# Decoder trunk on one core: gate, q and k turned and stored one token tile at a time, their splits and the scores in later slots, three more warming matmuls

## The chip, the core and the metric

The kernel runs on one core of a Trainium2 chip. The metric is the device time of one execution in microseconds; lower is better. The engines are named as in the profile: PE is TensorE (PEld its weight loads), DVE is VectorE, ACT is ScalarE, POOL is GpSimd and SP is SyncE. Each engine works through its own instructions in a fixed order and waits where an input is not there; POOL and SP also issue DMAs, in that order.

## What is computed

A trunk of two layers over 256 tokens of width 2048, in float32. In each layer:

```
h = rmsnorm(x, g) @ w_in            # columns: q, k, v and a gate z
q, k = rope(q), rope(k)
o = attention(q, k, v)              # per head, causal
x = x + (o * silu(z)) @ w_out
```

Layer 0 has two kinds of heads: 8 dilated heads (a mixture of three windows, which the kernel computes as one masked softmax), and 4 differential heads `(softmax(q1 k1) - lam * softmax(q2 k2)) @ v` with a norm behind them. Layer 1 has 16 causal heads. A last rmsnorm gives the output.

## The kernel before

**Slots and chunks.** The two layers are cut into 40 chunks of 512 output columns, in the order of `layer_chunks` (line 33): v, q, k, z for group 0, then q, k, z, v for groups 1 to 3, then four chunks of the output projection. A group is four heads (or two differential pairs). A chunk is 16 slots, one for each block of 128 of the 2048 inputs. Float32 products are made from three matmuls on parts rounded to a shorter format (high times high, high times low, low times high), and there are two token tiles of 128, so a slot is 6 matmuls of 128x512.

**Weights.** SP loads 1 MB pieces (`raw`, 3 buffers). `split(m)` (line 101) makes the parts of one 1024-column piece, enough for two slots: ACT writes `wh` (line 122), DVE writes `wl` (line 123). There are four buffers of each, so that the split for a slot pair 2m, 2m+1 can run only when the pair four earlier has been used; it is ahead of its use by six slots at most. In what follows a split "for slot s" is the one with 2m = s.

**Work in the slots.** Everything else is put into slots by `at(slot, f)` and runs after that slot's matmuls. What a chunk leaves is scheduled from `nxt`, the slot behind its end (lines 531 to 569). The Tile framework then orders the instructions of each engine by its own estimate of when inputs are ready, so an instruction can stand earlier or later than its slot; that order is fixed when the program is built.

**The path of q, k and z to the scores.** `evac_rope` (line 262) applies the rotation on DVE, four instructions for a token tile (lines 270 to 273), and `turn` (line 233) transposes 32x32 blocks (line 235). Both token tiles go into one tile `bz`; behind the second, `place` (line 238) stores it to DRAM by one DMA of 512 KB (`dt`, line 243) and reads it back transposed by eight DMAs of 64 KB (line 247), all on POOL, the loads waiting for the store to land. `split_rope` (line 278) splits q and k: ACT writes `qh`, `kh` (line 285), DVE `ql`, `kl` (line 286), one token tile after the other for k. `evac_z` (line 250) sends the gate along the same path to the tile `u`.

**Scores and products.** `softmax` (line 314) starts with a matmul on unsplit k and q of the first token tile (line 317) and goes on with three on the split parts. `attn_t` (line 349) transposes the probabilities through DRAM, a store `d` (line 356) and four loads `p` (line 360) for a head; `attn_h` splits them (`th`, `tl`, lines 369 and 370); `attn_o` and `diff_o` multiply by v; `finish_y` (line 384) multiplies by the gate and writes `yh`, `yl`, which the output projection reads. Evacuations are put at nxt and nxt + 2, the split of q and k at nxt + 13, the scores of a head at nxt + 14 and on.

**The start.** `WARM` (line 26) matmuls of 128x128 on ones (line 137) run on PE while the first loads are under way. Each is two passes, so the profile counts 20.

Of the kernel before, what the change touches and what calls it, by code (L numbers as in the profile page):

```python
# [8 lines left out]
F32 = mybir.dt.float32  # L9
# [6 lines left out]
P = 128  # L16
S = 256
# [5 lines left out]
SCALE = HD ** -0.5  # L23
LAM_INIT = 0.8 - 0.6 * math.exp(-0.3 * 0)
AHEAD = 3
WARM = 10
RAW_BUFS = 3
SPLIT_BUFS = 4
ALIGN = 512
# [23 lines left out]
def trunk(ctx, tc, x_nat, x_t, w0, o0, w1, o1, g0, g1, gfin, lam, subln, cos_t, sin_t,  # L53
          mask_d, mask_c, ident_in, out):
    nc = tc.nc
# [6 lines left out]
    work = ctx.enter_context(tc.tile_pool(name="work", bufs=1))  # L62
# [3 lines left out]
    dram = ctx.enter_context(tc.tile_pool(name="dram", bufs=2, space=bass.MemoryType.DRAM))  # L66
# [68 lines left out]
    pw = patt.tile([P, P], F32, tag="O", name="pw")  # L135
    for i in range(WARM):
        nc.tensor.matmul(pw, ones, ones, start=True, stop=True)
# [5 lines left out]
    def xr(kt):  # L143
        return xraw[kt // 4][:, kt % 4]
# [13 lines left out]
    md = const.tile([P, 3 * P], F32, name="md")  # L158
    mc = const.tile([P, 3 * P], F32, name="mc")
# [67 lines left out]
    def at(slot, f, *a):  # L227
        fill.setdefault(slot, []).append((f, a))

    yh, yl = [], []  # L230
    U, Q, K, V = {}, {}, {}, {}

    def turn(src, bt, tt):

        nc.vector.transpose(bt[:, :, tt].rearrange("p c h j -> p h c j"),  # L235
                            src.rearrange("p (h c j) -> p h c j", h=4, c=4))

    def place(bt, name):


        t = work.tile([P, 2, 4, 4, 32], F32, tag=name, name=name)
        d = dram.tile([P, 4, S], F32, tag="dt", name="dt")
        nc.gpsimd.dma_start(d, bt.rearrange("p c t h j -> p c (t h j)"))  # L243
        dv = d.rearrange("(a i) c (t x) -> c t i a x", a=4, t=2)
        for tt in range(2):
            for c in range(4):
                nc.gpsimd.dma_start(t[32 * c:32 * c + 32, tt].rearrange("p a h j -> p a (h j)"), dv[c, tt])  # L247
        return t

    def evac_z(ps, layer, g, tt, box):  # L250
        if tt == 0:
            box["bt"] = work.tile([P, 4, 2, 4, 32], F32, tag="bz", name="bz")
        z = work.tile([P, CW], F32, tag="t1", name="zt")
        th = work.tile([P, CW], F32, tag="t2", name="zth")
        nc.scalar.activation(z, ps[:, tt], AF.Copy, scale=rn[:, tt:tt + 1])
        nc.scalar.activation(th, z, AF.Tanh, scale=0.5)
        nc.vector.scalar_tensor_tensor(z, th, 1.0, z, op0=ALU.add, op1=ALU.mult)
        turn(z, box["bt"], tt)
        if tt == 1:
            U[layer, g] = place(box["bt"], "u")  # L260

    def evac_rope(ps, name, store, layer, g, tt, box):
        if tt == 0:
            box["bt"] = work.tile([P, 4, 2, 4, 32], F32, tag="bz", name="bz")
        t1 = work.tile([P, CW], F32, tag="t1", name="rt1")
        t2 = work.tile([P, CW], F32, tag="t2", name="rt2")
        r, n = rn[:, tt:tt + 1], HD // 2
        p4, a4, b4 = (x.rearrange("p (h d) -> p h d", h=4) for x in (ps[:, tt], t1, t2))
        co, si = (x[:, tt, None, :].to_broadcast([P, 4, HD]) for x in (cosN, sinN))
        nc.vector.scalar_tensor_tensor(a4, p4, r, co, op0=ALU.mult, op1=ALU.mult)  # L270
        nc.vector.scalar_tensor_tensor(b4[:, :, 0:n], p4[:, :, n:HD], r, si[:, :, 0:n], op0=ALU.mult, op1=ALU.mult)
        nc.vector.scalar_tensor_tensor(b4[:, :, n:HD], p4[:, :, 0:n], r, si[:, :, n:HD], op0=ALU.mult, op1=ALU.mult)
        nc.vector.tensor_add(t1, t1, t2)
        turn(t1, box["bt"], tt)
        if tt == 1:
            box["t"] = place(box["bt"], name)

    def split_rope(name, store, layer, g, box):

# [233 lines left out]
    for (kind, layer, g), slot0 in list(zip(chunks, starts))[:-1]:  # L513
        ps = pacc.tile([P, 2, CW], F32, tag="acc", name=f"acc{slot0}")
        nxt = slot0 + KT
        for slot in range(slot0, nxt):
            if slot % 2 == 0:
                split(slot // 2 + AHEAD)
                load((slot // 2 + AHEAD) // 2 + 1)
            if layer == 0 and slot < KT and 2 * AHEAD <= slot + 4 < KT:  # L520
                split_x(0, slot + 4, xr(slot + 4))
            wh, wl = (x[slot % 2] for x in splits[slot // 2])
            kt = slot - slot0
            for b in range(2):
                bs = slice(b * P, (b + 1) * P)
                a_h, a_l = (yh[kt][:, bs], yl[kt][:, bs]) if kind == "o" else \
                    (xhl[kt][:, 0, bs], xhl[kt][:, 1, bs])
                mm3(ps[:, b], a_h, a_l, wh, wl, start=kt == 0, stop=kt == KT - 1)
            for f, a in fill.pop(slot, []):
                f(*a)  # L530
        if kind in "zqk":
            box = {}
            for tt in range(2):
                if kind == "z":
                    at(nxt + 2 * tt, evac_z, ps, layer, g, tt, box)
                else:
                    at(nxt + 2 * tt, evac_rope, ps, kind, (Q, K)[kind == "k"], layer, g, tt, box)
            if kind != "z":
                at(nxt + 13, split_rope, kind, (Q, K)[kind == "k"], layer, g, box)
            if kind != "k":  # L540
                continue
            if layer == 0 and g >= 2:
                for h in range(2):
                    box = {}
                    at(nxt + 14 + 6 * h, diff_s, layer, g, h, box, 0)
                    at(nxt + 16 + 6 * h, diff_s, layer, g, h, box, 1)
                    at(nxt + 18 + 6 * h, attn_t, box)
                    at(nxt + 32 + 5 * h, attn_h, box, True)
                    at(nxt + 34 + 5 * h, diff_o, layer, g, h, box)
                    at(nxt + 38 + 5 * h, diff_y, layer, g, h, box)  # L550
            else:
                for h in range(4):
                    box = {}
                    at(nxt + 14 + 3 * h, attn_s, layer, g, h, md if layer == 0 else mc, box)
                    at(nxt + 17 + 3 * h, attn_t, box)
                    at(nxt + 32 + 2 * h, attn_h, box)
                    at(nxt + 34 + 2 * h, attn_o, layer, g, h, box)
        elif kind == "v":
            if slot0 == 0:
                at(nxt + 5, evac_v, ps, layer, g)  # L560
            else:
                evac_v(ps, layer, g)
        else:
            evac_o(ps, layer, g)
            if layer == 0:
                at(nxt + 3, next_x, g, 0)
                at(nxt + 6, next_x, g, 1)
            else:
                at(nxt + 4, times_g, g)
# [64 lines left out]
```

## Time and profile before

| | us |
|---|---|
| median of 3 runs (lowest, highest) | 1003.44 (997.42, 1008.15) |
| the profiled execution's own time | 999.49 |
| its span, first to last instruction | 997.7 |
| PE busy | 942.4 |
| DVE busy | 643.0 |
| ACT busy | 474.5 |
| POOL busy | 200.5 |
| mean granted TensorE clock | 0.971 of full speed |

The profile is of one execution. Its span leaves out 1.8 us of its time. A group in the list of costliest groups gives the line, the engine, output and inputs, shape and count, then the busy time in us, the mean duration in ns, and the idle time just before these instructions with what ended it. Matmuls overlap, so the interval from one to the next, not their duration, is what they cost. In the timeline each row has the start, the duration, the engine and the instruction, with idle time before it in brackets. The rows on which the prediction rests stand in it.

### The profile page before, as it was taken

To read this page: it belongs to the slowest core of one execution; us is meant where nothing else is said; L and a number is where in the kernel's file an instruction comes from. 1 tells how busy PE (TensorE), PEld (TensorE's weight loads), DVE (VectorE), ACT (ScalarE), POOL (GpSimd) and SP (SyncE) were. 2 spreads that over 40 slices of the span, in tenths; PEclk is the share of its full clock that TensorE was granted. 3 is DMA by queue.
4 is the path that set the end of the run, shared out by engine and by line. 5 is a ranking of instruction groups with operands and counts; after the bars stand their busy time and mean duration, and the time that the engine had idled before them with its cause. 6 is when DMAs were issued, how large, how long until landed. Compare 5 with 4: busy or idle time off the path is not lost. (4 is left out here: it accounts for less than half of the span.)

```text
span 997.7 us, 11928 instructions
## 1 busy us (share of the span) xinstructions
PE 942.4 (94%) x4276; PEld 778.8 (78%) x4276; DVE 643.0 (64%) x999; ACT 474.5 (48%) x711; POOL 200.5 (20%) x368
## 2 busy tenths in 40 slices
PE   8999997999799988999999999979996999799996
PEld 7887886888688867888888878868885888587886
DVE  6666875756566666665555768747664766575572
ACT  7534643553355335554554454535442644264451
POOL 0021441321113110300000125215011421132000
PEclk9999999999989998999999999989997999899999
DMA  9786776566645664655555668667665756676542
GB/s 329 259 320 232 242 241 212 198 210 244 214 161 210 213 232 137 220 196 174 187 193 185 237 212 266 219 199 234 212 209 180 245 198 211 211 241 227 187 169 84
DMA packets 42827, 213.21 MB, mean 214 GB/s; under 512 B 9040, under 2 KB 9808, under 8 KB 22672
## 3 DMA queue, kind: packets, MB, share of 16 engines
q1 hardware_dynamic: 27504, 175.21, 50.1%
q0 software_dynamic: 14976, 36.20, 11.4%
q10 hardware_dynamic: 288, 1.05, 0.3%
q8 instruction: 33, 0.54, 0.2%
q14 instruction: 26, 0.21, 0.1%
HBM read 192.23 MB, written 20.19 MB: 213 GB/s over the span
## 5 line engine op out<-in xcount | busy, mean ns | idle before, releaser
L312 PE MATMUL acc<-wh,x 128*128 128x512 f32 x2048 | 655.1, 397 | 1.6 <-ACT wh L119 1.6
L123 DVE TENSOR_TENSOR wl<-raw,wh 128x1024 fp32r<-128x1024 f32 x314 | 382.7, 1220 | 206.1 <-ACT wh L122 205.3
L122 ACT ACTIVATE wh<-raw 128x1024 fp32r<-128x1024 f32 x314 | 332.0, 1059 | 359.8 <-PE acc L312 322.2
L312 PEld LDWEIGHTS acc<-wh,x 128*128 128x128 f32 x2048 | 390.7, 191 | 81.9 <-ACT wh L119 1.8
L312 PE MATMUL acc<-wl,x 128*128 128x512 f32 x1024 | 405.1, 396 | 0.2 <-DVE wl L120 0.2
L312 PEld LDWEIGHTS acc<-wl,x 128*128 128x128 f32 x1024 | 196.0, 191 | 39.8 <-DVE wl L120 0.5
L312 PE MATMUL acc<-wh,yh 128*128 128x512 f32 x224 | 88.3, 394 | 0.0
L312 PE MATMUL acc<-wl,yh 128*128 128x512 f32 x224 | 87.4, 390 | 0.0
L312 PE MATMUL acc<-wh,yl 128*128 128x512 f32 x224 | 87.3, 390 | 0.0
L243 POOL DMA_DIRECT2D dt<-bz x24 | 13.6, 568 | 305.6 <-DVE bz L235 302.1
L360 POOL DMA_DIRECT2D p<-d x112 | 61.2, 554 | 56.8 <-DMA d<-bt 29.5
L317 PE MATMUL ps_s<-k,q 128*128 128x128 f32 x64 | 14.7, 315 | 41.8 <-DMA k<-dt 41.6
L317 PEld LDWEIGHTS ps_s<-k,q 128*128 128x128 f32 x64 | 12.8, 214 | 47.0 <-issue 29.8
L312 PEld LDWEIGHTS acc<-wh,yl 128*128 128x128 f32 x224 | 42.0, 188 | 9.1 <-DVE yl L389 0.3
L312 PEld LDWEIGHTS acc<-wl,yh 128*128 128x128 f32 x224 | 42.1, 188 | 8.4
L312 PEld LDWEIGHTS acc<-wh,yh 128*128 128x128 f32 x224 | 42.1, 188 | 8.2
L247 POOL DMA_DIRECT2D q<-dt x64 | 34.7, 550 | 39.2 <-ACT wh L122 19.7
L247 POOL DMA_DIRECT2D k<-dt x64 | 34.7, 549 | 32.6 <-DMA dt<-bz 19.6
L356 POOL DMA_DIRECT2D d<-bt x28 | 15.7, 561 | 124.3 <-DVE st L328 85.6
L247 POOL DMA_DIRECT2D u<-dt x64 | 34.7, 549 | 19.0 <-DMA p<-d 13.2
L286 DVE TENSOR_TENSOR kl<-k,kh 128x512 fp32r<-128x512 f32 x16 | 11.0, 688 | 39.1 <-ACT kh L285 39.1
L285 ACT ACTIVATE kh<-k 128x512 fp32r<-128x512 f32 x16 | 10.0, 624 | 44.3 <-DMA k<-dt 44.2
(122 smaller groups left out, 663.8 us busy)
## 6 DMA issues: line engine op xcount, KB each, us to landing
raw<-in_w SPq DMA_DIRECT2D x124, 1024.0 KB, 5.2
raw<-in_o SPq DMA_DIRECT2D x32, 1024.0 KB, 4.8
dt<-bz POOLq DMA_DIRECT2D x24, 512.0 KB, 4.2
d<-bt POOLq DMA_DIRECT2D x28, 192.0 KB, 4.3
p<-d POOLq DMA_DIRECT2D x112, 48.0 KB, 4.7
q<-dt POOLq DMA_DIRECT2D x64, 64.0 KB, 3.6
k<-dt POOLq DMA_DIRECT2D x64, 64.0 KB, 6.2
u<-dt POOLq DMA_DIRECT2D x64, 64.0 KB, 4.6
```

Source lines behind the costliest of these rows:

```text
L122: nc.scalar.activation(ht, r, AF.Copy)
L123: nc.vector.tensor_sub(lt, r, ht.bitcast(F32))
L243: nc.gpsimd.dma_start(d, bt.rearrange("p c t h j -> p c (t h j)"))
L247: nc.gpsimd.dma_start(t[32 * c:32 * c + 32, tt].rearrange("p a h j -> p a (h j)"), dv[c, tt])
L285: nc.scalar.activation(a, v, AF.Copy)
L286: nc.vector.tensor_sub(b, v, a.bitcast(F32))
L312: nc.tensor.matmul(out_, l, r, start=start and i == 0, stop=stop and i == 2)
L317: nc.tensor.matmul(ps[:, 0:P], q[:, h * P:(h + 1) * P], k[:, 0, :, h], start=True, stop=True)
L356: nc.gpsimd.dma_start(d, bt.rearrange("p c b j -> p c (b j)"))
L360: nc.gpsimd.dma_start(pt[32 * c:32 * c + 32], dv[c])
```

## The change

`turn` and `place` become one function. Each token tile gets its own `bz` (two buffers of half the size) and its own store of 256 KB (four DRAM buffers in place of two); behind the second, the eight loads are written as before. The second token tile is evacuated one slot after the first, not two. The split of q and k goes from nxt + 13 to nxt + 18. The scores start at `first` = nxt + 22, and at nxt + 20 for group 3, in place of nxt + 14, and the transposes, splits and products behind them move with them at new distances. `WARM` goes from 10 to 13. No arithmetic is changed.

```diff
-WARM = 10
+WARM = 13
...
-    def turn(src, bt, tt):
-        nc.vector.transpose(bt[:, :, tt].rearrange("p c h j -> p h c j"),
-                            src.rearrange("p (h c j) -> p h c j", h=4, c=4))
-
-    def place(bt, name):
-        t = work.tile([P, 2, 4, 4, 32], F32, tag=name, name=name)
-        d = dram.tile([P, 4, S], F32, tag="dt", name="dt")
-        nc.gpsimd.dma_start(d, bt.rearrange("p c t h j -> p c (t h j)"))
-        dv = d.rearrange("(a i) c (t x) -> c t i a x", a=4, t=2)
-        for tt in range(2):
-            for c in range(4):
-                nc.gpsimd.dma_start(t[32 * c:32 * c + 32, tt].rearrange("p a h j -> p a (h j)"), dv[c, tt])
-        return t
+    def turn(src, box, name):
+        tt = len(box)
+        bt = work.tile([P, 4, 4, 32], F32, tag="bz", name="bz", bufs=2)
+        nc.vector.transpose(bt.rearrange("p c h j -> p h c j"), src.rearrange("p (h c j) -> p h c j", h=4, c=4))
+        d = dram.tile([P, 4, P], F32, tag="dt", name="dt", bufs=4)
+        nc.gpsimd.dma_start(d, bt.rearrange("p c h j -> p c (h j)"))
+        box[tt] = d.rearrange("(a i) c x -> c i a x", a=4)
+        if tt == 1:
+            box["t"] = t = work.tile([P, 2, 4, 4, 32], F32, tag=name, name=name)
+            for i in range(2):
+                for c in range(4):
+                    nc.gpsimd.dma_start(t[32 * c:32 * c + 32, i].rearrange("p a h j -> p a (h j)"), box[i][c])
...
-                    at(nxt + 2 * tt, evac_z, ps, layer, g, tt, box)
+                    at(nxt + tt, evac_z, ps, layer, g, tt, box)
                 else:
-                    at(nxt + 2 * tt, evac_rope, ps, kind, (Q, K)[kind == "k"], layer, g, tt, box)
+                    at(nxt + tt, evac_rope, ps, kind, (Q, K)[kind == "k"], layer, g, tt, box)
             if kind != "z":
-                at(nxt + 13, split_rope, kind, (Q, K)[kind == "k"], layer, g, box)
+                at(nxt + 18, split_rope, kind, (Q, K)[kind == "k"], layer, g, box)
...
+            late = g == 3
+            first = nxt + (20 if late else 22)
             if layer == 0 and g >= 2:
                 for h in range(2):
                     box = {}
-                    at(nxt + 14 + 6 * h, diff_s, layer, g, h, box, 0)
-                    at(nxt + 16 + 6 * h, diff_s, layer, g, h, box, 1)
-                    at(nxt + 18 + 6 * h, attn_t, box)
-                    at(nxt + 32 + 5 * h, attn_h, box, True)
-                    at(nxt + 34 + 5 * h, diff_o, layer, g, h, box)
-                    at(nxt + 38 + 5 * h, diff_y, layer, g, h, box)
+                    at(first + 5 * h, diff_s, layer, g, h, box, 0)
+                    at(first + 2 + 5 * h, diff_s, layer, g, h, box, 1)
+                    at(first + 4 + 5 * h, attn_t, box)
+                    at(first + 15 + 5 * h, attn_h, box, True)
+                    at(first + 16 + 5 * h, diff_o, layer, g, h, box)
+                    at(first + 20 + 4 * h, diff_y, layer, g, h, box)
             else:
                 for h in range(4):
                     box = {}
-                    at(nxt + 14 + 3 * h, attn_s, layer, g, h, md if layer == 0 else mc, box)
-                    at(nxt + 17 + 3 * h, attn_t, box)
-                    at(nxt + 32 + 2 * h, attn_h, box)
-                    at(nxt + 34 + 2 * h, attn_o, layer, g, h, box)
+                    at(first + 3 * h, attn_s, layer, g, h, md if layer == 0 else mc, box)
+                    at(first + 3 + 3 * h, attn_t, box)
+                    at(first + (13 if late else 15) + 3 * h, attn_h, box)
+                    at(first + (15 if late else 17) + 3 * h, attn_o, layer, g, h, box)
```

**Where PE meets the first scores.** The first head of group 1, layer 0, whose k chunk ends at slot 96. `acc` is the chunk's sum in PSUM, `x_101` to `x_116` (`x_104` to `x_119` with the change) are the 16 blocks of the input, one for each slot. Before, on PE:

```order
L312 MATMUL acc_1330<-wh_1425,x_115 128x512
L317 MATMUL ps_s<-k,q 128x128
L312 MATMUL acc_1330<-wh_1425,x_116 128x512
L312 MATMUL acc_1330<-wl_1426,x_116 128x512
```

With the change, one chunk on:

```order
L305 MATMUL acc_1511<-wh_1512,x_110 128x512
L310 MATMUL ps_s<-k,q 128x128
L305 MATMUL ps_s<-kh,qh 128x256
L305 MATMUL ps_s<-kl,qh 128x256
L305 MATMUL ps_s<-kh,ql 128x256
L305 MATMUL acc_1511<-wh_1512,x_111 128x512
```

The first score matmul stood behind 15 slots of the chunk that follows k; it stands behind 23 slots now, with the matmuls on the split parts right behind it. In group 3 of both layers it stands behind 21.

**Where ACT splits k.** The same group, on ACT. The number in `wh_` only counts up; consecutive rows are splits for consecutive slot pairs. Before:

```order
L122 ACTIVATE wh_1459<-raw_1411 128x1024
L122 ACTIVATE wh_1481<-raw_1445 128x1024
L285 ACTIVATE kh<-k 128x4x128
L122 ACTIVATE wh_1514<-raw_1445 128x1024
L285 ACTIVATE kh<-k 128x4x128
L255 ACTIVATE zt<-acc_1330,rn 128x512
```

With the change:

```order
L122 ACTIVATE wh_1443<-raw_1390 128x1024
L278 ACTIVATE kh<-k 128x4x128
L122 ACTIVATE wh_1459<-raw_1429 128x1024
L122 ACTIVATE wh_1477<-raw_1429 128x1024
L278 ACTIVATE kh<-k 128x4x128
L122 ACTIVATE wh_1493<-raw_1463 128x1024
```

Counted from the end of the k chunk, the first `kh` stood behind the split for slot 20 and the second behind that for slot 22. Now the first stands behind the split for slot 14, ahead of the one for slot 16, and the second behind that for slot 18, ahead of the one for slot 20. So the instruction was put into a later slot, and the order moved it up. It is so in all eight groups, and `kl` stands between the same `wl` on DVE.

**What POOL issues between groups 0 and 1 of layer 0.** `bz` and `dt` are the turned tile and its DRAM copy, here of q of group 1; `bt`, `d` and `p` belong to the probabilities of the last head of group 0. Before:

```order
L356 DMA d_1054<-bt_1052 128x384
L243 DMA dt_1166<-bz_1117 128x1024
L360 DMA p_1016<-d_1054 32x4x96 x4
L247 DMA q_1165<-dt_1166 32x4x128 x8
```

With the change:

```order
L241 DMA dt_1123<-bz_1121 128x512
L349 DMA d_1164<-bt_1162 128x384
L247 DMA q_1141<-dt_1123 32x4x128
L241 DMA dt_1139<-bz_1137 128x512
L247 DMA q_1141<-dt_1123 32x4x128 x3
L247 DMA q_1141<-dt_1139 32x4x128 x4
L353 DMA p_1096<-d_1164 32x4x96 x4
```

The store of the first token tile goes out ahead, and four of the eight loads wait for it alone. The last head's four `p` loads stood ahead of the eight q loads and stand behind them now. Between groups 0 and 1 of layer 1 it is the same.

More of the change, by code (lines that the diff above doesn't have):

```diff
@@ L231, in trunk @@
     U, Q, K, V = {}, {}, {}, {}
-    def turn(src, bt, tt):
-        nc.vector.transpose(bt[:, :, tt].rearrange("p c h j -> p h c j"),
-                            src.rearrange("p (h c j) -> p h c j", h=4, c=4))
-    def place(bt, name):
-        t = work.tile([P, 2, 4, 4, 32], F32, tag=name, name=name)
-        d = dram.tile([P, 4, S], F32, tag="dt", name="dt")
-        nc.gpsimd.dma_start(d, bt.rearrange("p c t h j -> p c (t h j)"))
-        dv = d.rearrange("(a i) c (t x) -> c t i a x", a=4, t=2)
-        for tt in range(2):
-            for c in range(4):
-                nc.gpsimd.dma_start(t[32 * c:32 * c + 32, tt].rearrange("p a h j -> p a (h j)"), dv[c, tt])
-        return t
+    def turn(src, box, name):
[10 more added lines that the diff above has]
+                    nc.gpsimd.dma_start(t[32 * c:32 * c + 32, i].rearrange("p a h j -> p a (h j)"), box[i][c])
     def evac_z(ps, layer, g, tt, box):
-        if tt == 0:
-            box["bt"] = work.tile([P, 4, 2, 4, 32], F32, tag="bz", name="bz")
         z = work.tile([P, CW], F32, tag="t1", name="zt")
@@ L257, in evac_z @@
         nc.vector.scalar_tensor_tensor(z, th, 1.0, z, op0=ALU.add, op1=ALU.mult)
-        turn(z, box["bt"], tt)
+        turn(z, box, "u")
         if tt == 1:
-            U[layer, g] = place(box["bt"], "u")
+            U[layer, g] = box["t"]
     def evac_rope(ps, name, store, layer, g, tt, box):
-        if tt == 0:
-            box["bt"] = work.tile([P, 4, 2, 4, 32], F32, tag="bz", name="bz")
         t1 = work.tile([P, CW], F32, tag="t1", name="rt1")
@@ L273, in evac_rope @@
         nc.vector.tensor_add(t1, t1, t2)
-        turn(t1, box["bt"], tt)
-        if tt == 1:
-            box["t"] = place(box["bt"], name)
+        turn(t1, box, name)
     def split_rope(name, store, layer, g, box):
```

## The prediction

> **What bounds the kernel now.** I read the page first: the shares of the engines, then the clock by slices.
>
> ```profile
> span 997.7 us, 11928 instructions
> ...
> PE 942.4 (94%) x4276; PEld 778.8 (78%) x4276; DVE 643.0 (64%) x999; ACT 474.5 (48%) x711; POOL 200.5 (20%) x368
> ...
> PEclk9999999999989998999999999989997999899999
> ```
>
> PE is the bound: it is busy 94% of the span. No other engine needs to get faster; what can be won is PE's idle time, 55.3 us, and the slices in which its clock fell. So the next view is the list of waits, for the waits of PE and for what else waits for the same thing, and then the group of score matmuls:
>
> ```profile
> PE ps_s L317 <- DMA k<-dt: 41.6, 7, 7.9
> ...
> DVE ql L286 <- ACT qh L285: 15.4, 7, 2.8
> ```
>
> ```profile
> L312 PE MATMUL ps_s<-kh,qh 128*128 128x256 f32 x32 | 10.2, 329 | 1.8 <-ACT kh L285 1.8
> ```
>
> Three quarters of PE's idle time is one wait: the first score matmul of a group stands in PE's queue while k is still on its way through DRAM, and all the projection matmuls behind it wait too. Seven of the eight groups have it, and the eighth (group 0 of layer 1) has most of the 1.8 us for the split k. Together that is 41.6 + 1.8 = 43.4 us. The timeline of PE at the worst one (group 3, layer 0) shows a second loss:
>
> ```profile
> 378.05 0.80 PE L317 MATMUL ps_s<-k,q 128*128 128x128 f32 x2 [7.67 <-DMA k<-dt]
> ...
> 379.50 1.05 PE L312 MATMUL acc<-wh,x 128*128 128x512 f32 x2
> 380.35 0.63 PE L312 MATMUL acc<-wl,x 128*128 128x512 f32 x1
> ...
> 387.58 0.61 PE L312 MATMUL acc<-wh,x 128*128 128x512 f32 x2
> 388.03 0.39 PE L312 MATMUL acc<-wl,x 128*128 128x512 f32 x1
> 388.26 0.61 PE L312 MATMUL acc<-wh,x 128*128 128x512 f32 x2
> ```
>
> Compare starts. From 387.58 to 388.26 three matmuls take 0.68 us, so a slot of six takes 1.36 us. Behind the stall two take 0.85 us (379.50 to 380.35): half speed. Windows of 10 us from the end of each long stall, with the granted clock as the last column but two, price this:
>
> ```profile
> 174.20:184.20 10.00, 9.95 (x40) 8.31 (x41) 5.96 (x17) 6.59 (x16) 0.00 (x0) 0.80 0.33 113
> 274.80:284.80 10.00, 9.92 (x37) 8.20 (x38) 5.07 (x15) 5.46 (x12) 0.00 (x0) 0.71 0.30 106
> 378.00:388.00 10.00, 9.95 (x38) 8.27 (x39) 5.45 (x15) 5.95 (x13) 0.00 (x0) 0.75 0.31 106
> ...
> 664.30:674.30 10.00, 9.96 (x38) 8.25 (x39) 5.33 (x16) 5.94 (x12) 0.00 (x0) 0.73 0.32 114
> 767.30:777.30 10.00, 9.94 (x39) 8.26 (x40) 5.58 (x17) 6.23 (x14) 0.00 (x0) 0.76 0.30 105
> 868.90:878.90 10.00, 9.98 (x37) 8.26 (x38) 5.24 (x16) 6.01 (x12) 0.00 (x0) 0.72 0.30 105
> ```
>
> What is missing from 1.00, times 10 us, is lost work: 2.0 + 2.9 + 2.5 + 2.7 + 2.4 + 2.8 = 15.3 us, 2.55 us for a long stall. The two groups with short waits lose none.
>
> **The later scores take the wait away: 43.4 + 15.3 = 58.7 us.** Take the worst group. These rows of DVE and POOL show when k came; the chunk ended at 350.0, where the first rotation starts:
>
> ```profile
> 350.01 0.75 DVE L270 SCALAR_TENSOR_TENSOR rt<-acc,rn,cosN 128x512 f32<-128x512 f32 x1 [0.40 <-PE acc L312]
> ```
>
> ```profile
> 358.33 0.70 DVE L235 STREAM_TRANSPOSE bz<-rt 128x512 f32<-128x512 f32 x1
> ...
> 363.39 0.70 DVE L235 STREAM_TRANSPOSE bz<-rt 128x512 f32<-128x512 f32 x1
> ```
>
> ```profile
> 364.39 0.56 POOL L243 DMA_DIRECT2D dt<-bz  x1 [16.71 <-DVE bz L235]
> 368.65 4.33 POOL L247 DMA_DIRECT2D k<-dt  x8 [3.70 <-DMA dt<-bz]
> ```
>
> The first k half was there 28.0 us behind the chunk's end (378.05), that is 20.6 slots; the scores asked for it at 15 slots. They ask at 23 now (31.3 us), and at 21 in group 3 (28.6 us): even an unchanged path would be in time. PE's instructions are the same in number but for the warming ones, so what is left of the span without these stalls is 997.7 - 58.7 = 939.0 us. That a denser PE would lose clock by itself isn't seen: the slices without a stall, 17 to 23 of the clock's row above all, read 9.
>
> **The splits stand earlier than their slots: 0 to 16 us, I take 3.2.** ACT and DVE wait for k now, with the weight splits for slot 16 queued behind the first `kh`, `kl`, and those for slot 20 behind the second. If these are late, PE starves. The rows for the durations and the landings:
>
> ```profile
> L123 DVE TENSOR_TENSOR wl<-raw,wh 128x1024 fp32r<-128x1024 f32 x314 | 382.7, 1220 | 206.1 <-ACT wh L122 205.3
> L122 ACT ACTIVATE wh<-raw 128x1024 fp32r<-128x1024 f32 x314 | 332.0, 1059 | 359.8 <-PE acc L312 322.2
> ...
> L285 ACT ACTIVATE kh<-k 128x512 fp32r<-128x512 f32 x16 | 10.0, 624 | 44.3 <-DMA k<-dt 44.2
> ```
>
> ```profile
> dt<-bz POOLq DMA_DIRECT2D x24, 512.0 KB, 4.2
> d<-bt POOLq DMA_DIRECT2D x28, 192.0 KB, 4.3
> p<-d POOLq DMA_DIRECT2D x112, 48.0 KB, 4.7
> ```
>
> ```profile
> DMA to landing us min/median/max: 2.2/6.2/8.3
> ```
>
> Behind k's landing come `kh` 0.62, `wh` 1.06 and `wl` 1.22, 2.9 us. `wl` is first needed one matmul (0.23) into its slot: 16 x 1.36 + 0.23 - 2.9 = 19.1 us behind the chunk's end is the first half's deadline, 20 x 1.36 + 0.23 - 2.9 = 24.5 us the second's.
>
> Now the new path. Before, the two transposes ended 9.0 and 14.1 us behind the chunk's end. DVE loses its wait for `ql` (15.4 us in seven, 2.2 each, since q's split stands behind q's landing by then), and one `wl` stands less ahead of the second transpose: 14.1 - 2.2 - 1.2 = 10.7 us; the first is at about 6. Store at 6.0, landed 4.2 later at 10.2; four loads at 0.55 (4.33 for eight) until 12.4; second store there (its tile is ready at 10.7), landed at 16.6; four loads until 18.8, the last issued at 18.25. With k's landings of 2.2, 6.2 and 8.3 us the first half is there at 14.1, 18.1 or 20.2, against 19.1; the second at 20.5, 24.4 or 26.5, against 24.5. So nothing at the median, 2.0 us a group at the worst. I take 0.4 a group, 3.2 us in eight, near the median because the halves compete with half as many loads. If this cover is gone, each us later costs 8 us. The other `dt` halves (q, u) have the same loads; q's split waits at a deadline like k's second half, and the gate is asked for some 20 slots on. The 24 added stores cost POOL 24 x 0.57 = 13.6 us, on an engine that is busy 20%.
>
> The Trainium skill ("DMA: Bandwidth & Descriptors", the anatomy of a GpSimd DMA) fits such a DMA as 2.0 us plus its bytes at 436 KB per us; by that a store of half the size would land 0.6 us sooner. The rows speak against it here, 192 KB taking 4.3 us and 512 KB 4.2, and I count nothing for it; by the page the second half would have 0.6 us to spare and the 3.2 us would go towards 1.
>
> **The products with v: 0 to 8 us, I take 2.** Twelve slots (16.3 us) from transpose to split hold the store, its landing (4.3), four loads and theirs (4.7), some 12 us. The one place where more is queued ahead is the last head of group 0 in both layers: its `p` loads wait behind q's eight. By the path above q's last load is out 18.8 us behind q's chunk, the `p` loads at 21.0, landed at 25.2. PE asks at slot 98 of the program, 18 slots behind that chunk (24.5 us, and some 2 us of attention matmuls in between). About 1 us each, up to 4.
>
> **The ends.** At the end of layer 0 the last `yh` is made one slot closer to its use: 0 to 2 us, I take 1. At the start three matmuls add six passes of 0.2 us to a row that ends at 5.0, with PE idle until 6.6:
>
> ```profile
> 1.06 3.95 PE L137 MATMUL pw<-ones 128*128 128x128 f32 x20 [1.06 <-DVE fs L463]
> 6.62 0.49 PE L312 MATMUL acc<-wh,x 128*128 128x512 f32 x1 [1.61 <-ACT wh L119]
> ```
>
> They end at 6.2 and delay nothing. If the clock rises earlier, the next weights limit the gain to 1 us; I take 0.3.
>
> **The sum.** 997.7 - 58.7 + 3.2 + 2 + 1 - 0.3 = 944.9 us of span; with the 1.8 us around it 946.7 us, against the profiled execution's 999.49. The three runs went from 997.42 to 1008.15, so that about 1% can be told from no change, and their median lies 4 us above the profiled one. The forecast is 947 us.
>
> **The rivals.**
> 1. *The wait moves into the weight splits.* The second half of k lands 26.5 us or more behind the chunk. For it: `kh` stands ahead of the split for slot 20 everywhere, and in the group shown the landing took 7.7 us from the fourth load (370.3) on. Against it: the eight loads shared the queues then. 8 x 2.0 to 8 x 3.5 in place of 3.2: so 960 to 972 us.
> 2. *The products wait.* Both last heads of group 0 wait 4 us and PE falls to half speed behind it: 2 x (4 + 2.55) in place of 2, 958 us. Against it: `p` landed in 4.7 us at the median.
> 3. *The half speed stays,* by other short idle times: 946.7 + 15.3 = 962 us. Against it: the two short waits cost no clock.
> 4. *Slower.* The first half lands no sooner than k did before, at 28.0 us, since POOL, in order, holds the loads behind another landing. PE then starves at slot 16: 28.0 - 19.1 = 8.9 us and 2.55 of clock in eight groups, 92 us against 58.7 won: 1032 us. It decides from 19.1 + 58.7 / 8 = 26.4 us on. Against it: the first store leaves at about 6 us, not at 14.4.
> 5. *The change does not do what it says:* the first halves come no sooner and the scores alone are later. The splits that stand earlier then starve PE as in rival 4, with its 1032 us. Against it: the order has four loads ahead of the second store.
>
> **How the numbers follow.** The forecast 0.75, rivals 1, 2 and 3 0.10, 0.07 and 0.04, rivals 4 and 5 0.02, something unseen that leaves it within 1% 0.02. All of the first four lie more than 1% under 999: faster 0.96, same 0.02, slower 0.02. The range for 8 in 10 goes from the sum with no new wait and the start's whole us (939.0 + 1.8 - 1 = 940), less 3 for a faster execution, to the upper bounds of splits and products (939.0 + 1.8 + 16 + 8 + 1 = 966): 937 to 966 us.
>
> **What would show it.** Right: no wait of line 310 (317 before) for k in the list; PE busy for about 99% of the span; granted clock near 1.00 but for the start; `kh` waiting for k with PE still running. Wrong: PE waiting for `wh` or `wl` of lines 122 and 123 at slots 16 and 20 behind a k chunk (rivals 1, 4), for `th` or `tl` at slot 98 and 418 (rival 2), or slices of clock under 0.9 in the middle (rival 3).

## The result, and the profile after

The changed kernel took 960.14 us at the median (952.38 to 965.63, four executions) beside 1000.43 for the kernel before on the same chip: a ratio of 0.958, 95% interval 0.948 to 0.968. Two later measurements gave 957.09 and 954.66 us; the median of all fourteen executions is 955.9 us. One execution of the kernel with the slots alone (below) took 3325 us and one of the kernel before beside it 1897 us; ratios and ranges leave such slow executions out. The forecast was 947 us, the range 937 to 966.

The profiled execution is the quickest of the first four, 952.38 us. Its page, then the list of PE's waits (total, times, longest), then the two windows of 10 us behind its longest waits, with the granted clock as the last column but two:

```profile
span 950.6 us, 11999 instructions
...
PE 928.7 (98%) x4282; PEld 772.6 (81%) x4282; DVE 645.7 (68%) x999; ACT 470.8 (50%) x711; POOL 214.2 (23%) x392
...
PEclk9999998999999999999999999999999999999999
```

```profile
PE po L305 <- ACT th L362: 8.7, 2, 5.4
PE acc L305 <- DVE wl L123: 1.7, 3, 1.1
PE po L305 <- DVE y L380: 1.3, 1, 1.3
...
PE acc L305 <- DVE wl L120: 0.4, 2, 0.2
PE acc L305 <- ACT wh L119: 0.4, 1, 0.4
```

```profile
156.20:166.20 10.00, 10.00 (x34) 8.24 (x35) 8.30 (x13) 3.05 (x5) 2.74 (x5) 0.70 0.45 151
...
622.70:632.70 10.00, 9.97 (x39) 8.31 (x40) 8.74 (x14) 3.78 (x5) 3.19 (x6) 0.83 0.53 156
```

No wait for k is left, and the five dips in the clock's row have become one. A wait stands first that was 0.5 us before: PE for `th`, in front of the products with v.

The difference of the spans, 997.7 - 950.6 = 47.1 us, falls into 33.4 us of PE's idle time (55.3 to 21.9) and 13.7 us of its busy time (942.4 to 928.7). The idle part closes: 43.4 us for k are gone, the start is 1.0 us shorter, the products wait 10.0 us where they waited 0.8, the weight splits 1.7 where they waited none: 43.4 + 1.0 - 9.2 - 1.7 = 33.5. Of the busy part, the clock explains 12.2 us: summed over windows of 5 us, 16.3 us of work were lost to it before and 4.1 now. 1.5 us are left over.

ACT waits for k now where PE did; in this group row the idle time ahead of the instructions and its cause stand at the end:

```profile
L278 ACT ACTIVATE kh<-k 128x512 fp32r<-128x512 f32 x16 | 10.1, 631 | 52.1 <-DMA k<-dt 52.1
```

These 52.1 us cost PE next to nothing. In group 3 of layer 0, the prediction's worst, the path reads like this, DVE first, then ACT, then the first score matmul on PE:

```profile
342.87 0.74 DVE L265 SCALAR_TENSOR_TENSOR rt<-acc,rn,cosN 128x512 f32<-128x512 f32 x1
```

```profile
357.55 0.63 ACT L278 ACTIVATE kh<-k 128x512 fp32r<-128x512 f32 x1 [3.53 <-DMA k<-dt]
...
363.29 0.63 ACT L278 ACTIVATE kh<-k 128x512 fp32r<-128x512 f32 x1 [3.21 <-DMA k<-dt]
```

```profile
370.44 0.38 PE L310 MATMUL ps_s<-k,q 128*128 128x128 f32 x2
```

The first half was read 14.7 us behind the start of the rotation, the second 20.4, and PE asked at 27.6.

### The profile page after: what moved, and what is told of

The parts are those of the page before. It is cut to its first block, busy times and chain, and to the rows that moved or that the text cites. A ratio compares the mean times of both kernels' runs of the same rounds, so it can differ in the third digit from the quotient of the medians.

```text
span 950.6 us, 11999 instructions
## 1 busy us (share of the span) xinstructions
PE 928.7 (98%) x4282; PEld 772.6 (81%) x4282; DVE 645.7 (68%) x999; ACT 470.8 (50%) x711; POOL 214.2 (23%) x392
## 3 DMA queue, kind: packets, MB, share of 16 engines
q10 hardware_dynamic: 288, 1.05, 0.4%
## 4 chain that ended last, share of the span: by engine, by line
PE 76%; DMA 9%; issue 6%; DVE 3%; POOL 3%; ACT 1%; SPq 0%; ACTq 0%; POOLq 0%; DVEq 0%
PE acc L305 71%; DMA dt<-bz 5%; DMA p<-d 2%; PE last L468 1%; DVE wl L123 1%; POOL q L247 1%; DMA d<-bt 1%; PE ps_s L305 1%; PE po L305 1%; DMA q<-dt 1%; POOL k L247 1%; DMA raw<-in_w 1%; PE ps_s L310 1%; PE po L389 0%; DVE bz L239 0%
## 5 line engine op out<-in xcount | busy, mean ns | idle before, releaser
L305 PE MATMUL acc<-wh,x 128*128 128x512 f32 x2048 | 646.5, 392 | 0.4 <-ACT wh L119 0.4
L305 PEld LDWEIGHTS acc<-wh,x 128*128 128x128 f32 x2048 | 386.2, 189 | 79.5 <-ACT wh L119 0.9
L305 PE MATMUL acc<-wl,x 128*128 128x512 f32 x1024 | 401.0, 392 | 2.3 <-DVE wl L123 1.7
L305 PEld LDWEIGHTS acc<-wl,x 128*128 128x128 f32 x1024 | 193.2, 189 | 43.3 <-DVE wl L123 4.2
L241 POOL DMA_DIRECT2D dt<-bz x48 | 27.2, 566 | 259.5 <-DVE bz L239 259.3
L247 POOL DMA_DIRECT2D q<-dt x64 | 34.9, 552 | 56.4 <-DMA dt<-bz 47.1
L319 ACT ACTIVATE p<-p,st 128x128 f32<-128x128 f32 x64 | 28.5, 446 | 30.2 <-DVE st L315 30.2
L278 ACT ACTIVATE kh<-k 128x512 fp32r<-128x512 f32 x16 | 10.1, 631 | 52.1 <-DMA k<-dt 52.1
L362 ACT ACTIVATE th<-p 128x256 fp32r<-128x256 f32 (+1 forms) x28 | 12.0, 429 | 45.2 <-DMA p<-d 45.2
```

Of the source, the lines that this page charges most:

```text
L241: nc.gpsimd.dma_start(d, bt.rearrange("p c h j -> p c (h j)"))
L247: nc.gpsimd.dma_start(t[32 * c:32 * c + 32, i].rearrange("p a h j -> p a (h j)"), box[i][c])
L278: nc.scalar.activation(a, v, AF.Copy)
L305: nc.tensor.matmul(out_, l, r, start=start and i == 0, stop=stop and i == 2)
L319: nc.scalar.activation(p[:, sl], p[:, sl], AF.Exp, bias=st[:, 0, i:i + 1], scale=-1.0, accum_out=st[:, 1, i:i + 1])
L362: nc.scalar.activation(th4, pt[:, 0:n], AF.Copy)
```

## The experiments

**Which part takes the wait for k away?** The halves alone, with the scores, transposes and products where they were:

```diff
-            first = nxt + (20 if late else 22)
...
-                    at(first + 3 * h, attn_s, layer, g, h, md if layer == 0 else mc, box)
+                    at(nxt + 14 + 3 * h, attn_s, layer, g, h, md if layer == 0 else mc, box)
```

> The two stores of half the size and the evacuations of the change, but scores, transposes and products at the slots of before (scores from the 14th slot behind the chunk of k); the split of k stands where the change has it among the weight splits. Theory A (the shorter path wins about two thirds of the wait for k by itself, the later scores the rest): by the landings in the profile of the changed kernel the first half of k comes 13.7 to 18.0 us behind its chunk and the second 19.0 to 24.2, so that kl is ready at 20.3 to 25.5 us; PE asks at 20.9. Waits of 0 to 4.6 us in front of the split scores, some 14 us in eight groups, one or two of them with half speed behind (3 us). The loads of p of the last head of group 0 stand ahead of the next q here, so the 14.8 us lost there in the changed kernel fall to under 2: 952 + 14 + 3 - 13 = 956 us, between 948 and 968. Rival: the halves gain little without the later scores, since q or the second half still comes 26 us or more behind the chunk: waits of 5 us and more in most groups, 980 us or more.

Measured: 971.32 us (967.12 to 977.39), ratio 0.972 (0.965 to 0.979). The list of PE's waits in this kernel:

```profile
PE ps_s L305 <- ACT kh L278: 13.0, 6, 4.8
PE po L305 <- ACT th L362: 2.7, 2, 1.6
PE po L305 <- DVE y L380: 1.7, 3, 0.8
PE ps_s L305 <- DVE kl L279: 1.4, 4, 0.3
```

The wait for k came as worked out, 14.4 us, and the wait for `th` fell to 2.7. The median is 15 us above the expectation all the same, and the profiled execution, the quickest at 967.12 us, 11 us. In that profile the lost clock is 5.0 us where 3 were counted, PE waits 2.7 us for `th` in other groups, and other short waits take a microsecond more; but some 5 us are PE's busy time beyond what the clock explains (934.5 against 928.7 us in the change, with 5.0 and 4.1 us of clock), and these are not settled. Now the slots alone, with the old `turn` and `place` and their one store of 512 KB:

```diff
-                    at(nxt + tt, evac_rope, ps, kind, (Q, K)[kind == "k"], layer, g, tt, box)
+                    at(nxt + 2 * tt, evac_rope, ps, kind, (Q, K)[kind == "k"], layer, g, tt, box)
...
-        nc.gpsimd.dma_start(d, bt.rearrange("p c h j -> p c (h j)"))
+        nc.gpsimd.dma_start(d, bt.rearrange("p c t h j -> p c (t h j)"))
```

> The later slots and the three warming matmuls of the change, but one store of 512 KB for both token tiles as before. Theory A (the scores only had to come later; a path as long as before is in time): k came 20.5 + 5.9 = 26.4 us behind its chunk on average before, 28.0 us at the worst, and is asked for at 28.6 to 31.3 us. The split of k stands in ACT's order ahead of the weight splits for the 22nd and 24th slot here, whose deadlines are 22 x 1.36 + 0.23 - 2.9 = 27.3 and 30.0 us: PE starves by under 1 us a group for some of them. The loads of p of the last head of group 0 stand ahead of the next q, so no wait as in the changed kernel: 940 to 950 us, faster than the change. Rival (the halves are what makes it work): ACT and DVE wait for k until 28 us and more, PE starves 2 to 9 us in each group and falls to half speed behind it: 975 to 1030 us.

Measured: 966.22, 969.28 and 972.78 us, ratio 0.970 (0.962 to 0.977). PE's waits, and the last group's k, from the start of its rotation on DVE to ACT's first split:

```profile
PE po L312 <- ACT th L369: 4.0, 2, 2.1
PE pdo L312 <- ACT th L369: 3.4, 1, 3.4
PE acc L312 <- DVE wl L123: 3.0, 6, 0.8
PE ps_s L312 <- ACT kh L285: 2.2, 1, 2.2
...
PE ps_s L317 <- DMA k<-dt: 0.8, 1, 0.8
```

```profile
806.48 0.75 DVE L270 SCALAR_TENSOR_TENSOR rt<-acc,rn,cosN 128x512 f32<-128x512 f32 x1 [0.40 <-PE acc L312]
```

```profile
836.71 0.63 ACT L285 ACTIVATE kh<-k 128x512 fp32r<-128x512 f32 x1 [9.13 <-DMA k<-dt]
```

With `kl` (0.4) the wait for k is 3.4 us in place of 43.4, though k came as late as before, 20.0 to 30.2 us behind. So the later slots alone take nearly all of this wait away. PE is hardly starved by the weight splits here (3.0 + 0.7 us for `wl` and `wh`), but this doesn't test rival 5: `kh` stands ahead of the split for slot 22 in this kernel, not for slot 16 as in the change. What rules out rival 5 and its 1032 us is the change's own profile, in which the first halves did come sooner. The time is still 16 us or more over the expected 950: 7.4 us of waits for `th`, other short waits and 7.7 us of clock were not in it. By the ratios either part alone wins 28 to 31 us and both together 44: they remove mostly the same wait, so their gains don't add.

**Where is what is left?** The change itself, twice more:

> The changed kernel once more. In its first profile (952.38 us) PE waited 5.35 + 3.40 us for th, in front of the products of the last head of group 0 in both layers, 1.3 us ahead of the head before, and ran below full speed for 3.0 + 1.7 us behind these, 14.8 us in all; the other executions took 956 to 966 us. Theory A: what is left of lost PE time, and what differs from one execution to the next, sits at these two places. The new profile then shows the same two waits, longer if the time is longer, no wait for k, and its time less these waits and the clock behind them is 937 to 940 us. Rival B: the difference comes from landings anywhere; the two waits stay at 5 and 3 us and waits for wl, wh or k in other groups, or clock below 1.00 in other slices, make up the rest.

> The changed kernel once more, beside the three that follow. By its eight times so far 952 to 966 us, median 957 to 960; the list of waits with th of the last head of group 0 first (8 to 10 us in two places), wl second, no k.

Measured: 957.09 (952.52 to 960.86) and 954.66 us (951.73 to 958.94). The waits of the second profile, whose span is 959.1 us:

```profile
PE po L305 <- ACT th L362: 12.5, 4, 5.9
PE acc L305 <- DVE wl L123: 3.8, 8, 1.2
PE po L305 <- DVE y L380: 1.3, 1, 1.3
```

The two waits at the last head of group 0 are there again (5.87 and 4.13 us, 5.59 and 3.88 in the third), with 4.1 and 3.6 us of lost clock. So these two waits come in every profile of the change. Of the 8.5 us by which this execution is longer only 1.2 are in them: 2.5 us are waits for `th` in the last group, 2.6 waits for weight splits, and 2.9 more busy time. On the spread the rival was right.

Why is `th` late? On ACT the split of the next q stands ahead of it, and on POOL the loads of p stand behind that q's eight. First the order on ACT alone:

```diff
+    after_t = []
...
+    def split_after(*a):
+        with tc.issue_after(after_t[-1]):
+            split_rope(*a)
...
-            nc.scalar.activation(t.rearrange("p (a j) -> p a j", a=4), pt[:, 2], AF.Copy)
+            after_t.append(nc.scalar.activation(t.rearrange("p (a j) -> p a j", a=4), pt[:, 2], AF.Copy).ins)
...
-                at(nxt + 18, split_rope, kind, (Q, K)[kind == "k"], layer, g, box)
+                at(nxt + 18, split_after if kind == "q" and g == 1 else split_rope, kind, (Q, K)[kind == "k"], layer, g, box)
```

> The changed kernel with one order changed: on ACT the split of q of group 1 stands behind th and t of the last head of group 0, not ahead of them. In the two profiles of the change PE waited 5.35 and 5.87 us (layer 0), 3.40 and 4.13 us (layer 1) there. Theory A (p itself is late): its four loads were issued at 146.6 to 148.5 behind q's eight and took 5.9 to 6.4 us, so they landed at 152.5 to 155, and th started at 155.72: the wait shrinks by 1 us at most in either layer, the time stays within 3 us of the change. Theory B (qh, which waited 5.79 us for q, holds th back): the wait falls under 2 us and the half speed behind it goes, 10 us less than the change.

Measured: 959.23 us (958.12 to 962.05). PE at the two places:

```profile
156.29 0.58 PE L310 MATMUL po<-th,vh 128*128 128x256 f32 x1 [4.52 <-ACT th L367]
...
626.72 0.58 PE L310 MATMUL po<-th,vh 128*128 128x256 f32 x1 [3.09 <-ACT th L367]
```

The waits shrank by 0.3 to 1.4 us: `qh` is not what holds `th` back, p is late. The trace of the change shows why, from the end of q's chunk in both views. PE at that end (the last row is the next chunk), then DVE, ACT and POOL behind it:

```profile
120.37 0.38 PE L310 MATMUL ps_s<-k,q 128*128 128x128 f32 x2
...
120.94 0.40 PE L305 MATMUL acc<-wh,x 128*128 128x512 f32 x1
```

```profile
123.07 0.58 DVE L347 STREAM_TRANSPOSE bt<-p 128x384 f32<-128x384 f32 x1 [3.98 <-DMA d<-bt]
...
127.73 0.43 DVE L363 TENSOR_TENSOR tl<-p,th 128x256 fp32r<-128x256 f32 x1 [2.98 <-ACT th L362]
128.07 0.75 DVE L265 SCALAR_TENSOR_TENSOR rt<-acc,rn,cosN 128x512 f32<-128x512 f32 x1
```

```profile
127.28 0.42 ACT L362 ACTIVATE th<-p 128x256 fp32r<-128x256 f32 x1 [8.02 <-DMA p<-d]
```

```profile
144.47 2.17 POOL L247 DMA_DIRECT2D q<-dt  x4 [2.30 <-DMA dt<-bz]
146.63 1.63 POOL L353 DMA_DIRECT2D p<-d  x3
148.50 0.55 POOL L353 DMA_DIRECT2D p<-d  x1 [0.23 <-DMA q<-dt]
```

The next chunk began at 120.94; q's rotation began at 128.07, 7.1 us later. Before, the same rotation followed its chunk at once, after 0.35 us of waiting for PE:

```profile
123.30 0.75 DVE L270 SCALAR_TENSOR_TENSOR rt<-acc,rn,cosN 128x512 f32<-128x512 f32 x1 [0.35 <-PE acc L312]
```

In the change DVE stood 3.98 us for a buffer `bt`, whose store had to land (from 119.09 on, so in part ahead of the chunk's end), and 2.98 us behind the first head's `th`, which waited 8.02 us for its p. Without these 7.0 us it would have reached the rotation at 121.1. So the stores, q's loads and the loads of p behind them are all late; these landed in 5.9 to 6.4 us, the last not before 154.4, and `th` started at 155.72.

Next, everything of the first three groups two slots earlier, which puts p's loads ahead of q's:

```diff
-            first = nxt + (20 if late else 22)
+            first = nxt + 20
```

> The changed kernel with the scores from nxt + 20 in every group, not in group 3 alone; the products of the first three groups come two slots earlier with them. So the stores and loads of p of the last head of group 0 stand ahead of the loads of the next q on POOL, and th ahead of qh on ACT. Theory A (the last heads of group 0 are what is left): the waits for th of 5.35, 3.40 and 1.3 us and the 4.7 us of clock behind them go, 952.4 - 14.8 = 938 us against the profile of the change, 938 to 944; k's second half with kl is there at 25.5 us at the latest and is asked for at 28.6, so no new wait. Rival B (the rest is spread over the groups): 948 us or more, with waits at other places. Rival C (the wait only moves on): q's loads are now behind p's, q lands later, and ql or the weight splits behind qh make PE wait in group 1: 945 to 955 us.

Measured: 954.24 us (951.01 to 959.73), the same as the change. The waits of its profile, which is its slowest execution, and DVE in group 0:

```profile
PE po L305 <- DVE y L380: 6.2, 3, 3.0
PE ps_yt L415 <- DVE yb L406: 4.6, 3, 2.3
PE acc L305 <- DVE wl L123: 3.3, 5, 1.4
...
PE pdo L305 <- ACT th L362: 0.2, 1, 0.2
```

```profile
128.97 0.43 DVE L363 TENSOR_TENSOR tl<-p,th 128x256 fp32r<-128x256 f32 x1 [4.53 <-DMA d<-bt]
```

The wait for `th` is gone and 3.0 us for `y` stand in its place, in both layers, and PE waits 4.6 us for `yb` of the differential heads, where the three profiles of the change have none. DVE still stands 4.53 us for the first head: the row names its store `d`, and on ACT `th` waited 4.61 us for the p read from it, until 128.52. That the wait for `y` comes from DVE's queue behind this is likely, but not shown. Rival C, then: the wait moved on, though to `y` and `yb` and not to the `ql` and weight splits that it named.

All four heads' splits and products of group 0 six slots later:

```diff
+                    more = 6 if g == 0 else 0
-                    at(first + (13 if late else 15) + 3 * h, attn_h, box)
-                    at(first + (15 if late else 17) + 3 * h, attn_o, layer, g, h, box)
+                    at(first + (13 if late else 15) + 3 * h + more, attn_h, box)
+                    at(first + (15 if late else 17) + 3 * h + more, attn_o, layer, g, h, box)
```

> As the kernel with only the last head later, but all four heads of group 0 have the split of p and the products 6 slots later. In the profile of the change th of the first head waited 8.02 us for p and held DVE up for 2.98 us (tl), just before the rotation of the next q; that is where q's delay began. Theory C (the jam of group 0 begins at the first head): DVE doesn't stall before the rotation, q lands earlier, the waits for th go as well as the 1.3 us for y: 940 to 944 us. Rival (what stands later now collides with the path of k of group 1, whose first rotation starts at 154 us): y, ql or kl late, waits of 1 to 3 us in groups 1, 948 us or more.

Measured: 956.63 us (953.37 to 966.65). The edit moved PE's products but not the start of the jam: the Tile framework left `tl` of the first head ahead of the rotation on DVE, which in layer 0 waited 3.44 us for `bt` and 2.85 us for `th` there as before, and the third head's product waited 4.20 and 3.82 us for `y` in the two layers. So this kernel tests nothing about the first head. The last head alone, against that kernel:

```diff
-                    more = 6 if g == 0 else 0
+                    more = 6 if g == 0 and h == 3 else 0
```

> The changed kernel with the split of p and the products of the last head of group 0, in both layers, 6 slots (8.2 us) later. Theory A (only that head asks too early): the waits of 5.35 to 5.87 and 3.40 to 4.13 us and the 4.1 us of half speed behind them go, 13 us less than the change: 957 - 13 = 944 us, and the list of waits keeps 1.3 us for y and 2 to 4 us for wl. Rival (the wait moves: DVE and ACT are behind there, and the next to come late is the weight split behind qh or the split of k of group 1): 950 us or more, with wl or kl in place of th.

> The kernel with only the last head of group 0 later by 6 slots, once more: 945 to 950 us as in its four times so far. Theory A, that the two waits for th and the half speed behind them are what the change still loses there (13 to 14 us): 9 to 13 us less than the change on the same chip. Rival (the first measurement was luck, since the change itself goes from 952 to 966): within 5 us of the change.

Measured: 948.51 us (945.43 to 949.62), ratio 0.947 (0.943 to 0.950), and 948.85 us (946.06 to 949.83), ratio 0.950 (0.945 to 0.954), where the change beside it had 0.957 (0.952 to 0.961). The second profile:

```profile
PE acc L305 <- DVE wl L123: 4.9, 10, 0.8
PE po L305 <- DVE y L380: 2.9, 2, 1.5
PE po L305 <- ACT th L362: 1.5, 1, 1.5
```

Both waits are gone. All ten executions lie under the quickest of the change's fourteen; on one chip the gain is 954.66 - 948.85 = 5.8 us. That is less than the 9 to 13 us expected, and only just more than the 5 us of the rival, though the waits and their clock came to 13 us. In its profile 1.7 us more for `wl` (4.9 against 3.2) and 1.7 us of clock behind the wait of 1.5 us take 3.4 us of it. Another 2.2 us come from the choice of execution: the two profiled ones are 8.0 us apart (957.65 and 949.68 us), the medians 5.8. The last 1.7 us are not settled. This is the fastest version found.

Is it the neighbour? In group 0 alone the chunk of q follows that of z at once; in the other groups v lies between, which needs no rotation and no DMA. So group 0 in the order q, k, z, v:

```diff
-        c += [(kind, g) for kind in ("vqkz" if g == 0 else "qkzv")]
+        c += [(kind, g) for kind in "qkzv"]
...
-                    at(nxt + tt, evac_rope, ps, kind, (Q, K)[kind == "k"], layer, g, tt, box)
+                    at(nxt + tt + (8 if slot0 == 0 else 0), evac_rope, ps, kind, (Q, K)[kind == "k"], layer, g, tt, box)
...
-                at(nxt + 18, split_rope, kind, (Q, K)[kind == "k"], layer, g, box)
+                at(nxt + (26 if slot0 == 0 else 18), split_rope, kind, (Q, K)[kind == "k"], layer, g, box)
```

> The changed kernel with the chunks of group 0 in the order q, k, z, v, as in the other groups, in both layers (the first rotation 8 slots and the first split of q 8 slots later, since rn and cos come only then). In the change the loads of p and the products of group 0 alone fall on the rotation and the eight loads of the next q, since no v stands between z and q. Theory C (that neighbour makes group 0 slow): no wait for th, y or tl at group 0 in either layer and no half speed: 957 - 15 = 942 us, between 938 and 947, with only the 3 us for wl and 2 to 3 us of th in the last group left. Rival (the first head waits for p in every group, 4 us, and group 0 is only where it shows first): the waits come back in other places and the time is 950 us or more. The start may cost up to 2 us, since the rotation falls into the stretch in which the weights' loads limit PE.

Measured: 954.37 us (950.85 to 962.23). The waits of 5.4 and 3.4 us for `th` are gone: the last head waits in neither layer, and PE's one wait for `th` left is 0.43 us at the second head of layer 1. In layer 0 q's rotation now starts as soon as PE has finished the chunk, where it was 7.1 us late:

```profile
136.49 0.75 DVE L265 SCALAR_TENSOR_TENSOR rt<-acc,rn,cosN 128x512 f32<-128x512 f32 x1 [0.63 <-PE acc L305]
```

DVE still stands 4.87 us for `bt` and 4.23 us for the first head's `th` in layer 0, but that ends 20 us ahead of the rotation. In layer 1 q's rotation is as late as it was (3.0 us, 3.2 before), but the last head's loads of p no longer stand behind q's: they are out at 593.9, and q's begin at 609.2. So the neighbour is the cause of the wait for `th` in both layers, by POOL's queue, and of the late rotation in layer 0. The time (expected: 942 us) didn't fall, because the start of layer 0 pays for it: ACT waits there for the first q and for the first p, with weight splits queued behind, and PE waits 2.32 and 2.95 us for `wh`, with 5.6 us of clock behind them, some 11 of the 12 us over the expectation:

```profile
67.58 0.63 ACT L278 ACTIVATE qh<-q 128x512 fp32r<-128x512 f32 x1 [10.47 <-DMA q<-dt]
...
115.06 0.42 ACT L362 ACTIVATE th<-p 128x256 fp32r<-128x256 f32 x1 [10.17 <-DMA p<-d]
```

Both together, the new order in layer 1 alone and the later head in layer 0 alone:

```diff
-        c += [(kind, g) for kind in ("vqkz" if g == 0 else "qkzv")]
+        c += [(kind, g) for kind in ("vqkz" if g == 0 and layer == 0 else "qkzv")]
...
+                    more = 6 if layer == 0 and g == 0 and h == 3 else 0
```

> The last head 6 slots later in layer 0 alone, and in layer 1 the chunks of group 0 in the order q, k, z, v. Theory C (group 0 is slow since the next q follows z at once): layer 1 has no wait for th or y at group 0, as in the kernel with v behind z in both layers, and layer 0 none as in the kernel with the last head later: 943 to 949 us, the same as that kernel or up to 3 us less. Rival (the order of layer 1 costs something that the other kernel's start hid): 950 us or more.

Measured: 953.87 us (946.80 to 958.98), and not under 949 as expected. Its profile, of the slowest execution, has no wait for `th` in layer 1, but `qh` of group 1 waited 9.79 us for q there, where POOL had waited 5.4 us for the second store to land, and the weight split behind it came 1.64 us late. What makes this kernel vary so much more than the last one is not settled.

**The start.** The change with ten warming matmuls:

```diff
-WARM = 13
+WARM = 10
```

> The change with ten warming matmuls as before. The clock of the first window of 25 us was 0.93 before and 1.00 with thirteen, and the first rotation, behind two chunks, started at 53.09 before and at 52.31 and 52.40 with the change. If the three matmuls made that: clock about 0.93 again and first rotation at 53.0 to 53.1. If the earlier start came from jitter of the first loads: clock 1.00 or the rotation at 52.3 to 52.6 with ten as well. The time can't tell 0.7 us from none.

Measured: 954.91 us, one execution. Its first 25 us, and the first rotation:

```profile
0.00:25.00 25.00, 22.00 (x93) 18.02 (x94) 17.04 (x31) 19.73 (x32) 0.20 (x4) 1.00 0.89 334
```

```profile
52.73 0.75 DVE L265 SCALAR_TENSOR_TENSOR rt<-acc,rn,cosN 128x512 f32<-128x512 f32 x1 [0.40 <-PE acc L305]
```

The clock is 1.00 with ten as well, and the rotation starts between the two cases (53.09 before, 52.40 with the change; 53.01 with thirteen in the kernel with the halves alone). So the three matmuls can't be shown to bring anything.

## Why the prediction was right, and where it was wrong

- **The wait for k (43.4 us) and the clock behind it (15.3 us): right.** Both are gone. "Even an unchanged path would be in time" held but for 3.4 us.
- **The path of k: right in five groups of eight.** Counted from the start of the rotation on DVE, the first halves were split at 13.7 to 18.0 us (predicted 14.1 to 20.2), the second at 19.0 to 24.2 (20.5 to 26.5). But the deadlines of 19.1 and 24.5 us count from the end of the chunk, and the prediction started the path there. In the five groups 2 and 3 of both layers and 0 of layer 1 this held within 1.2 us, and both halves were in time (14.5 to 19.0 and 19.8 to 23.5 us behind the chunk's last matmul). In groups 0 and 1 of layer 0 and 1 of layer 1 the rotation began 5.8, 5.7 and 3.7 us behind it, and the halves were split at 20.1 to 21.2 and 24.8 to 29.9 us, past both deadlines. One step that failed here is "DVE loses its wait for `ql`": of 15.4 us it kept nearly all, with 6.6 us in one place, ahead of k's rotation in group 0 of layer 0:

```profile
DVE ql L279 <- ACT qh L278: 14.2, 6, 6.6
```

In group 1 of both layers DVE stood 5.4 and 3.6 us for `yh`, which ACT writes behind `qh`. PE starved for only 0.4 us behind these late halves, in group 0 of layer 0. In group 1 of both layers it stood itself for `th` behind the same chunk (5.35 and 3.40 us), which put the later slots off. Where that wait is gone, in the second profile with the last head later, the first half of group 1 of layer 0 came at 21.2 us again and PE did wait 0.59 us for `wl`, 2.9 us behind the split.
- **The splits (3.2 us): right in size, mostly by luck.** PE waited 1.7, 3.8 and 3.2 us for `wl` in the three profiles, but only 0.4, 0.8 and 1.4 us of that stand 2.9 us behind a split of k, as the term has it. The rest is elsewhere; in two of the three the longest wait (1.05 and 1.16 us) is in the jam of group 0.
- **The products with v (2 us): this is the term that failed.** It came to 9.2 us of added waits and 3.0 + 1.7 us of clock behind them, 13.9 us. The prediction named the place, the last head of group 0 in both layers, and the queue, p's loads behind q's eight. What was wrong is the sentence "by the path above q's last load is out 18.8 us behind q's chunk". That path was taken from group 3, where DVE is free when the chunk ends. In group 0 of layer 0 DVE was 7.1 us late, held by the attention that the change itself moves there, so the last load of p was out at 28.1 us in place of 21.0 and landed at 33.5 in place of 25.2; PE asked at 29.9. In layer 1 DVE was some 3 us late, and the load was out at 24 us and landed at 29. The landings of some 6 us, not 4.7, are the smaller part. Rival 2, with 13.1 us for this, described what happened and had a chance of 0.07; the likeliest case did not.
- **The end of layer 0 (1 us): none seen** in this profile (0.06 us between 400 and 425).
- **The start (0.3 us):** 0.7 us by the first rotation, not shown to come from the change.
- **The half-size store:** counted at nothing, and the rows agree. 256 KB landed in 4.2, 4.1 and 4.1 us in the three profiles, 512 KB in 4.2 before and 3.5 in the kernel with the slots alone (medians). The Trainium skill ("DMA: Bandwidth & Descriptors", the anatomy of a GpSimd DMA) would have the smaller one 0.6 us sooner; the measurements decide. By that figure the prediction gave the second half 0.6 us to spare; on its own path the second store waits for the first half's loads, so both stores count and it is 1.2 us. Nothing in the sum hangs on it.

The forecast lies 5 us under the profiled execution and 9 us under the median of the fourteen, and the range holds both. With 13.9 in place of 2, no end of layer 0, 1.7 for the splits and 0.7 for the start it is 939.0 + 1.7 + 13.9 - 0.7 + 1.8 = 955.7 us. That this is nearly the median of the fourteen is chance: these terms are read from the quick profiled execution, which took 952.38.

## What to carry to other kernels

When a stall is removed by moving its consumers to later slots, look at what else stands in those slots: here the attention of group 0 fell on the rotation and the loads of the next q, and a quarter of the gain went into a new wait. Check the predicted path of a transfer in the place with the busiest neighbours, not in the one with the longest old wait; every engine on the path has to be free when it starts. And here the consumer that asks last was the cheap thing to move: six slots for one head in each layer were worth 6 us.

## What the runs showed of the hardware

**A short wait can cost as much clock as a longer one.** In the kernel with v behind z in layer 1 and the later head, PE waited 1.31 us in one place and 2.34 us in another; the two PE rows, then the granted clock in the 5 us behind each:

```profile
141.49 0.43 PE L305 MATMUL po<-th,vh 128*128 128x256 f32 x1 [1.31 <-DVE y L380]
...
412.72 0.41 PE L415 MATMUL ps_yt<-ident,yb 128*128 128x128 f32 x2 [2.34 <-DVE yb L406]
```

```profile
141.50:146.50 5.00, 5.00 (x17) 4.18 (x18) 3.88 (x7) 2.91 (x5) 2.09 (x5) 0.66 0.91 307
412.80:417.80 5.00, 4.92 (x23) 3.61 (x24) 3.95 (x7) 1.70 (x3) 0.00 (x0) 1.00 0.53 179
```

The shorter wait was followed by 0.66, the longer by full speed; a wait of 1.31 us in the change's own profile (140.14) by full speed too. 0.66 over 5 us is 3.4 us at half speed, 1.7 us of work, and the same 0.66 stands behind waits of 1.47, 2.23 and 2.38 us in other kernels here. So the length of the wait alone doesn't decide. The Trainium skill ("TensorE: Matmul & The Clock Gate", on the two states and on how the oscillation bites) has a free-running window of about 3.4 us, which the length of these stretches fits; its rule that only gaps over some 3.4 us matter doesn't hold in these rows.

**The warming row isn't constant.** The twenty passes of ten matmuls took 3.95 us before, with half speed from 7.6 to 11 us, and 4.63 us in the kernel with ten warming matmuls, at full speed from 7.7 us on.
